# A two-layer streaming encoder step on one core: the first 24 projection units and their adaLN blocks rebuilt, and the dt unit in two passes

## The chip, the cores and the metric

The kernel runs on one core of a Trainium2 chip. The metric is the device time of one launch in microseconds (us). TensorE (PE) multiplies; VectorE (DVE), ScalarE (ACT) and GpSimd (POOL) do elementwise work; SyncE (SP) and POOL issue the DMAs.

## What is computed

A prompt of 256 tokens and a sample of 64 run together as T = 320 columns through two layers of width 2048. Layer 0 is a Mamba-2 mixer beside sliding-window attention, layer 1 a gated short convolution. All tensors are float32. What matters here is the head of layer 0:

```python
mod = jax.nn.silu(c) @ w_ada + b_ada
shift, scale, gate = jnp.split(mod[:, None, :], 3, axis=-1)
h = rms_norm(x, g_pre) * (1 + scale) + shift
z, xbc, dt_raw, q, k, v, g_att = jnp.split(h @ w_in, cuts, axis=-1)
dt = jax.nn.softplus(dt_raw + dt_bias)
```

`c` has one row for the prompt and one for the sample, so `mod` is a product of two rows with a 2048 x 6144 matrix (50 MB) per layer. The outputs of `h @ w_in` are cut into units of 128 columns.

## The kernel before

Activations lie transposed: 16 K tiles of 128 features by 320 tokens. A float32 product is made of three matmuls in a shorter format: weights and activations are split into a high and a low part (`split`, line 148: ScalarE copies the high part, VectorE subtracts), and `block` (line 152) issues high x high (line 169), high x low (line 170) and low x high (line 171) into one PSUM tile. A block of weights is 16 tiles of 128 x 128, in two halves of 8. Two halves are kept in a list of jobs ahead of TensorE (`LOOK`), so that the split runs before the matmuls; after every fourth tile a tick lets the side work go on.

The adaLN product has two forms. On TensorE (`ada_pe`, line 208) a quarter is a tile of 128 x 4 x 512 weights, 16 matmuls whose two useful rows of `cs` are padded to 32, so that four of them stand side by side in four column groups; four quarters are a block and give shift and scale for two K tiles, and `ada_end` (line 259) copies, transposes and adds. A float32 matmul shows as two records. On VectorE (`ada_side`, line 225) a block is summed in 16 steps, each of two multiply-adds on a 128 x 512 tile; `RATE_0` says how many steps a tick makes.

The first 24 units (k, v, and q and gate of two head pairs) need `h`, and `h` needs `mod`, which comes from 25 MB of weights. So they are not computed unit by unit: K is cut into pieces of 1, 1, 2, 4, 4, 4 tiles (`PIECES`), and each piece runs over all 24 units while the adaLN quarters of the next piece stand between the units. After a piece a unit's PSUM tile is added to its sum in SBUF (`start_unit`, line 395): by ScalarE (a copy, line 405) in piece 0, by VectorE (line 416) afterwards. The PSUM tiles are three banks of the pool `psm`.

K tiles 0 and 1 have adaLN weights of their own (`w0`, eight tiles of 512 KB), which `ada_first` (line 357) sums in two column groups, one for the shift and one for the scale. Tokens' squares are summed in two sums by ScalarE (line 325) and VectorE, joined, reduced over features with three matmuls (`by_token`), turned into 1/sqrt with integer operations and three rounds on VectorE (`rstd`, line 292) and spread with three matmuls (`r0b`). `modulate` (line 333) makes for each K tile: x times scale times rstd on VectorE (`mt`), the high half on ScalarE (`hh`, adds the shift), the low half on VectorE (`hl`).

A scheduler sets the order of each engine's instructions from the program's order and its own model; an engine then runs its queue strictly in that order. SP issues the weights' DMAs in its own fixed order; an issue waits until its buffer is free. The rest of the kernel, from line 459 on, runs units whole: attention, the dt unit (line 663: one unit with 32 useful columns, padded to 128), the SSM groups, the output products, and layer 1.

## Time and profile before

| | us |
|---|---|
| median of three runs (2165.87 to 2166.52) | 2166.22 |
| profiled execution, whole | 2171.02 |
| its span, first to last instruction | 2169.3 |
| TensorE busy in the span | 2124.2 (98%) |
| VectorE busy | 1412.8 (65%) |
| ScalarE busy | 884.9 (41%) |
| mean DMA rate over the span | 188 GB/s |

The profile is one execution. A matmul's busy time overlaps that of the next one, so busy shares of TensorE are upper bounds; starts tell its pace. Idle time is put down to what ended it. In stretches, PEclk is the share of the full clock of 2.4 GHz that TensorE was granted.

### The profile page before, as it was taken

How to read it: one execution, taken by the hardware profiler on the slowest of the kernel's cores; microseconds unless marked ns; L12 is line 12 of the kernel's file. 1: busy time of each engine (PE TensorE's matmuls, PEld its weight loads, DVE VectorE, ACT ScalarE, POOL GpSimd, SP SyncE). 2: the span in 40 equal slices, each digit the busy share in tenths (PEclk: the TensorE clock that was granted, in tenths of full speed). 3: DMA queues.
4: the chain of work that ended last, by engine and by line, in shares of the span. 5: the costliest groups of instructions: out<-in, count | busy, mean ns of one | idle time of the engine just before them, and what ended most of it. 6: DMA issues, size and time to landing. Idle time of an engine off the chain costs nothing.

```text
span 2169.3 us, 38007 instructions
## 1 busy us (share of the span) xinstructions
PE 2124.2 (98%) x15582; PEld 2056.5 (95%) x15582; DVE 1412.8 (65%) x2295; ACT 884.9 (41%) x1442; POOL 154.2 (7%) x370
## 2 busy tenths in 40 slices
PE   7999999999999999999999999999999999999997
PEld 6889999999999999997999999999999999999996
DVE  5876788897577878996755555555345554444444
ACT  5233455543465555355433333333333333333343
POOL 1000000000132223102000000000000000000001
PEclk9999999999999999999999999999999999999998
DMA  8886455466455556775554454545444454444441
GB/s 314 325 313 212 167 179 181 168 230 231 164 192 176 178 183 210 251 285 217 175 172 166 173 176 161 178 166 190 154 172 159 175 175 143 154 155 140 153 156 68
DMA packets 85758, 408.81 MB, mean 188 GB/s; under 512 B 10544, under 2 KB 11472, under 8 KB 46416
## 3 DMA queue, kind: packets, MB, share of 16 engines
q1 hardware_dynamic: 80496, 392.22, 51.8%
q0 software_dynamic: 5088, 14.16, 2.0%
q8 instruction: 122, 2.00, 0.4%
q14 instruction: 52, 0.43, 0.1%
HBM read 400.35 MB, written 5.99 MB: 187 GB/s over the span
## 4 chain that ended last, share of the span: by engine, by line
PE 90%; DVE 4%; DMA 2%; issue 1%; ACT 1%; POOL 1%; POOLq 0%; SPq 0%; DVEq 0%; ACTq 0%
PE pc L169 13%; PE pc L170 13%; PE pc L171 13%; PE px L169 3%; PE px L171 3%; PE px L170 3%; PE s L169 2%; PE s L171 2%; PE s L170 2%; PE pz L169 2%; PE pz L170 2%; PE poe L169 2%; PE pod L169 2%; PE pod L171 2%; PE poe L170 2%; PE pz L171 2%
## 5 line engine op out<-in xcount | busy, mean ns | idle before, releaser
L250 DVE SCALAR_TENSOR_TENSOR adac<-adas,cs,adac 128x512 f32<-128x512 f32 x420 | 300.2, 745 | 53.2 <-DMA adas<-in_wada 53.0
L956 POOL COPY ncc<-cp 128x2 f32<-128x2 f32 x32 | 6.0, 186 | 933.8 <-DVE cp L954 933.8
L219 PE MATMUL adap<-adaw,cs 128*32 128x128 f32 x1152 | 43.2, 284 | 3.5 <-DMA adaw<-in_wada 3.5
L219 PEld LDWEIGHTS adap<-adaw,cs 128*32 128x32 f32 x1152 | 31.6, 113 | 12.1 <-issue 6.3
L676 POOL COPY nca<-xp 128x3 f32<-128x3 f32 x24 | 22.3, 929 | 196.8 <-ACT xp L674 196.8
L961 DVE SCALAR_TENSOR_TENSOR cc<-cp,ccw,cc 128x322 f32<-128x322 f32 x64 | 35.3, 551 | 1.1
L512 ACT ACTIVATE pr<-s,mx 128x192 f32<-128x192 f32 (+2 forms) x80 | 29.8, 406 | 13.0 <-DVE mx L507 13.0
L710 ACT ACTIVATE sg<-sg,acum 128x128 f32<-128x128 f32 (+1 forms) x96 | 29.3, 376 | 12.9 <-POOL sg L702 12.9
L954 DVE TENSOR_TENSOR cp<-pc,u 128x256 f32<-128x256 f32 x31 | 13.2, 425 | 31.0 <-PE pc L171 30.8
L342 ACT ACTIVATE hh<-mt,mod 128x256 fp32r<-128x256 f32 x64 | 23.7, 419 | 20.9 <-DVE mt L341 20.7
L416 DVE TENSOR_TENSOR g<-s,g 128x320 f32<-128x320 f32 x40 | 19.0, 485 | 12.5 <-PE s L171 12.5
L681 DVE SCALAR_TENSOR_TENSOR cv<-xp,cw,cv 128x323 f32<-128x323 f32 x48 | 26.5, 552 | 0.6
L969 DVE TENSOR_TENSOR sgg<-pc,sgg 128x320 f32<-128x320 f32 x31 | 15.1, 488 | 17.4 <-PE pc L171 17.3
L879 DVE TENSOR_TENSOR oo<-poe,oo 128x320 f32<-128x320 f32 x16 | 7.9, 492 | 25.6 <-PE poe L171 25.6
L416 DVE TENSOR_TENSOR q<-s,q 128x320 f32<-128x320 f32 x40 | 18.9, 486 | 7.8 <-PE s L171 7.4
L702 POOL TENSOR_SCALAR_AFFINE_SELECT sg<-sg 128x512 f32<-128x512 f32 (+1 forms) x24 | 21.6, 911 | 30.0 <-DMA sg<-acs_b 29.9
L416 DVE TENSOR_TENSOR acc<-s,acc 128x320 f32<-128x320 f32 x32 | 15.3, 487 | 12.3 <-PE s L171 12.0
L363 PE MATMUL adaf<-w,cs 128*32 128x128 f32 x128 | 10.4, 311 | 12.8 <-ACT ss L325 12.6
L343 DVE SCALAR_TENSOR_TENSOR hl<-mt,mod,hh 128x256 fp32r<-128x256 f32 x64 | 21.5, 379 | 1.3 <-ACT hh L342 1.1
L363 PEld LDWEIGHTS adaf<-w,cs 128*32 128x32 f32 x128 | 8.1, 125 | 13.8 <-ACT ss L325 12.6
L263 ACT ACTIVATE adar_None<-adap 128x128 f32<-128x128 f32 x23 | 6.3, 273 | 34.8 <-PE adap L219 29.3
L512 ACT ACTIVATION_READ_ACCUMULATOR pr<-s,mx 128x1 f32 x80 | 17.9, 224 | 0.0
(2529 smaller groups left out, 8742.0 us busy)
## 6 DMA issues: line engine op xcount, KB each, us to landing
wc<-in_wio SPq DMA_DIRECT2D x124, 1024.0 KB, 4.9
adas<-in_wada SPq DMA_DIRECT2D x224, 256.0 KB, 5.9
adaw<-in_wada SPq DMA_DIRECT2D x36, 1024.0 KB, 7.0
wx<-in_wie SPq DMA_DIRECT2D x24, 1024.0 KB, 5.0
...
```

Source lines behind the costliest of these rows:

```text
L169: PE.matmul(ps, lhsT=wh[:, n, :], rhs=xh, start=st, stop=False)
L170: PE.matmul(ps, lhsT=wh[:, n, :], rhs=xl, start=False, stop=False)
L171: PE.matmul(ps, lhsT=wl[:, n, :], rhs=xh, start=False, stop=en)
L219: PE.matmul(ps[32 * q : 32 * q + 32, :], lhsT=cs[:, kt, :], rhs=(w[k] if raw else w[:, k, :])[:, 128 * q : 128 * q + 128], start=kt == 0, ...
L250: V.scalar_tensor_tensor(acc[s], w, c, acc[s], op0=ALU.mult, op1=ALU.add)
L342: S.activation(hi, t[:, a:b], AF.Identity, bias=sh)
L416: V.tensor_tensor(dst, ps, a, op=ALU.add)
L512: S.activation(pr[m][u // 2][:, u % 2, a : a + CH[c][2]], ss[m][u // 2][:, u % 2, a : a + CH[c][2]], AF.Exp, bias=mx[:, j, u : u + 1], sca ...
L676: G.tensor_copy(nca[:, ci, 0, :], xp[:, 256:259])
L681: V.scalar_tensor_tensor(cv, xp[:, n : n + 323], cw[:, ci, n : n + 1], cv, op0=ALU.mult, op1=ALU.add)
L710: S.activation(sgs[b][n][:, h, :], sgs[b][n][:, h, :], AF.Exp, bias=acum[0:nt, b, hd : hd + 1])
L961: V.scalar_tensor_tensor(cv, xp[:, m : m + 322], ccw[:, c, m : m + 1], cv, op0=ALU.mult, op1=ALU.add)
```

## The change

- **The first 24 units.** x is multiplied by rstd in place (`normal`); high half, and the low half's subtrahend, are then made from x with scale and shift on ScalarE (`shifted`; for K tiles 0 and 1 the subtrahend on VectorE). The adaLN quarters are fetched in halves of 512 KB into the buffers of the activations' pool and stand on TensorE in pairs, at places that `PAIRS` lists. Inside a half block the matmuls go K tile by K tile. PSUM tiles alternate over five banks of two pools. Units 20 to 23 stay in PSUM from piece 0 to piece 1, which begins with them.
- **TensorE's order** is that of the program from the first adaLN matmul to the end of the 24 units.
- **Tiles 0 and 1.** `ada_first` uses four column groups (even and odd K tiles apart), folded by a matmul with a doubled identity. The token sums are not joined but reduced in two steps; 1/sqrt uses ScalarE's square root.
- **Small loads** (key and value cache, sinks, convolution weights and others) are issued when the first unit of the last piece is done, and not at the start.
- **The dt unit.** The 32 useful columns' low parts are put beside their high parts (columns 32 to 63), so two passes, with the high and the low activations, give both sums; they are added where dt is transposed.
- The work pool has 19 buffers instead of 20; the side block begins in piece 2 at 0.36 steps per tick.

```diff
-SPE = 20
+SPE = 19
...
-RATE_0, RATE_A, RATE_B, RATE_C, RATE_D = 0.24, 0.55, 0.2, 0.6, 0.14
+RATE_0, RATE_A, RATE_B, RATE_C, RATE_D = 0.36, 0.55, 0.2, 0.6, 0.14
...
+    class PE:
+
+
+        @staticmethod
+        def matmul(*a, **k):
+            ins = nc.tensor.matmul(*a, **k)
+            return tc.keep_in_program_order(ins) if pin[0] else ins
...
+    def block(src, name, entries, h, pool=wp, order=None, parts=1):
...
-                for n, (get, kt, st, en, then) in enumerate(part):
+                for m, n in enumerate(order or range(8)):
+                    get, kt, st, en, then = part[n]
...
-    acc0 = sums[0]
-    V.tensor_tensor(acc0, acc0, sums[1], op=ALU.add)
...
+    def ada_first(t, ks, ps):
+
+        for kt in ks:
+            for q in range(2):
+                c = 64 * (kt % 2) + 32 * q
+                PE.matmul(ps[c : c + 32, :], lhsT=cs[:, kt, :],
+                          rhs=w0[4 * t + kt // 4][:, kt % 4, 128 * q : 128 * q + 128], start=kt < 2, stop=kt > 13)
+
+    pin[0] = True
+    ps0 = psa.tile([128, 128], F32, tag="ada", name="adaf0")
+    ada_first(0, range(4), ps0)
+    base = mean(by_token(sums[0], "ss0a", ones[:, 0:1]), D, "r0m")
+    ss = by_token(sums[1], "ss0t", ones[:, 0:1])
+    ada_first(0, range(4, 16), ps0)
+    rsp = rstd(ss, D, "r0", True, base)
+    ada_end(0, 0, ps0, 0)
...
+    def normal(kt, rs):
+        x = xin[kt // 4][:, kt % 4, :]
+        V.tensor_tensor(x, x, rs, op=ALU.mult)
+
+    def shifted(kt, h, late=True):
+
+        g, k = kt // 4, kt % 4
+        if k == 0:
+            h[0].append(gtile(f"hh0_{g}", F32R))
+            h[1].append(gtile(f"hl0_{g}", F32R))
+        t = stile([128, T], f"mt0_{kt}")
+        last = []
+        for s, a, b in SEGS:
+            sc, sh = mod[0][:, 1, kt, s : s + 1], mod[0][:, 0, kt, s : s + 1]
+            x, hi, lo = xin[g][:, k, a:b], h[0][g][:, k, a:b], h[1][g][:, k, a:b]
+            last.append((x, hi, lo, sc, sh, t[:, a:b]))
+            ih = S.activation(hi, x, AF.Identity, scale=sc, bias=sh)
+        for x, hi, lo, sc, sh, ts in last:
+            if late:
+                S.activation(ts, hi.bitcast(F32), AF.Identity, scale=-1.0, bias=sh)
+                il = V.scalar_tensor_tensor(lo, x, sc, ts, op0=ALU.mult, op1=ALU.add)
+            else:
+                V.tensor_scalar(ts, x, sc, sh, op0=ALU.mult, op1=ALU.add)
+                il = V.tensor_tensor(lo, ts, hi.bitcast(F32), op=ALU.subtract)
+        return ih, il
...
+    PAIRS = ((), (3, 10), (1, 6, 11, 16), (1, 6, 11, 16), (2, 9), ())
+    DEPTH = (2, 4, 4, 3, 3, 0)
+    first = [(0, b, sub) for b in range(1, 7) for sub in range(4)]
+    fetched, begun, carried = [], set(), {}
+
+    def ada_fetch(depth):
+
+        while first and len(fetched) < depth:
+            q = first.pop(0)
+            t = [act.tile([128, 2, 512], F32, tag="G", name=f"adaw{q[1]}_{q[2]}{m}") for m in range(2)]
+            for m in range(2):
+                nc.sync.dma_start(t[m], i["wada"][q[0], q[1], q[2]][:, 2 * m : 2 * m + 2, :])
+            fetched.append((q, [t[k // 2][:, k % 2, :] for k in range(4)]))
+
+    def ada_pair(depth):
+        for _ in range(2):
+            q, raw = fetched.pop(0)
+            ada_pe(*q, raw=raw)
+        ada_fetch(depth)
+        if q[2] == 3:
+            for kt in (2 * q[1], 2 * q[1] + 1):
+                shifted(kt, h0)
...
+            gate = G.dma_start(o["nk"][:, u, 0, :], kT[u][:, 128:256])
+            if u == 0:
+                with tc.issue_after(gate.ins):
+                    load_later()
...
+    normal(0, rsp)
+    behind = shifted(0, h0, False)
+    normal(1, rsp)
+    S.activation(rsb, rsp, AF.Copy)
+    banks = [0]
+
+    def bank(name):
+        banks[0] += 1
+        return mmps(name) if banks[0] % 5 < 3 else sps([128, T], name)
...
+        def then(n, ps, j=j, nxt=nxt, pairs=pairs, seen=seen):
+            c = seen[0]
+            seen[0] += 1
+            if not (j == 0 and n >= 20):
+                start_unit(n, ps, j == len(PIECES) - 1)
+            if j == 0 and c == 10:
+                ps1 = psa.tile([128, 128], F32, tag="ada", name="adaf1")
+                ada_first(1, range(16), ps1)
+                ada_end(0, 0, ps1, 1)
+                shifted(1, h0, False)
+                ada_fetch(DEPTH[1])
+            if c == 2 and nxt and j > 1:
+                for kt in range(nxt[0], nxt[0] + nxt[1]):
+                    normal(kt, rsb)
+            if c == 13 and j == 0:
+                for kt in (2, 3):
+                    normal(kt, rsb)
+            if pairs and c >= pairs[0]:
+                pairs.pop(0)
+                ada_pair(DEPTH[j])
+            if j == 2 and c == 8:
+                side["gen"], side["rate"] = ada_side([(0, 7)]), RATE_0
+            if j == 4 and c == 16:
                 finish_side()
-                modulate(xin, rsb, 0, *nxt, h0)
+                for kt in (14, 15):
+                    shifted(kt, h0)
...
+                keep = n >= 20 and j < 2
+                if keep and j:
+                    get = carried[n]
+                else:
+                    get = once(f"s{j}_{n}", bank)
+                    carried[n] = get
...
+            V.tensor_tensor(wh[:, :, 32:64], part[:, :, 0:32], wh[:, :, 0:32].bitcast(F32), op=ALU.subtract)
+
+            def mm(hf=hf, wh=wh):
+                ps = get()
+                for n in range(8):
+                    kt = 8 * hf + n
+                    for m in range(2):
+                        PE.matmul(ps[0:96], lhsT=wh[:, n, 0:96], rhs=h[m][kt // 4][:, kt % 4, :],
+                                  start=kt == 0 and m == 0, stop=kt == 15 and m == 1)
+                    if n % 4 == 3:
```

**TensorE at the start.** In the kernel before: `adaf` is tile 0's (218) or tile 1's (370) adaLN sum, `ss0t` the token sums, `r0b` the broadcast of rstd, `s_n` the PSUM tile of unit n, `hh` and `hl` the halves of the activations.

```order
L363 MATMUL adaf_218<-w_1_92,cs 32x128 x7
L313 MATMUL r0b<-r0d,ones 128x128 x2
L313 MATMUL r0b<-r0d,ones 128x64
L363 MATMUL adaf_218<-w_1_92,cs 32x128
L363 MATMUL adaf_218<-w_2_93,cs 32x128 x8
L363 MATMUL adaf_218<-w_3_94,cs 32x128 x8
L265 MATMUL adat_0_0_253<-ident,adar_0_0_251 128x64
L363 MATMUL adaf_370<-w_4_95,cs 32x128 x8
L363 MATMUL adaf_370<-w_5_96,cs 32x128 x5
L169 MATMUL s_0_319<-hh_0_296,ws00h_305 128x320
L169 MATMUL s_1_324<-hh_0_296,ws00h_305 128x320
L169 MATMUL s_2_329<-hh_0_296,ws00h_305 128x320
```

And after the change:

```order
L43 MATMUL adaf_193<-w_1_92,cs 32x128 x8
L43 MATMUL adaf_193<-w_2_93,cs 32x128 x8
L43 MATMUL adaf_193<-w_3_94,cs 32x128 x8
L43 MATMUL r0b<-r0d,ones 128x128 x2
L43 MATMUL r0b<-r0d,ones 128x64
L43 MATMUL adat_0_0_257<-fold,adar_0_0_255 128x64
L43 MATMUL s_0_320<-hh_0_286,ws00h_297 128x320
L43 MATMUL s_0_320<-hl_0_287,ws00h_297 128x320
L43 MATMUL s_0_320<-hh_0_286,ws00l_298 128x320
```

All of tile 0's adaLN stands ahead of the broadcast now, nothing of tile 1's stands ahead of the units, and the second matmul on unit 0 is the one with the low half.

**VectorE at the same place.** Before: `mt` is the scaled activation, `ws00l` and `ws01l` the low parts of the first weights, `hl` the low half of K tile 0.

```order
L341 SCALAR_TENSOR_TENSOR mt_0_298<-x_83,mod_134,rsb 128x256
L341 SCALAR_TENSOR_TENSOR mt_0_298<-x_83,mod_134,rsb 128x64
L150 TENSOR_TENSOR ws00l_306<-early_103,ws00h_305 128x1024
L150 TENSOR_TENSOR ws01l_310<-early_104,ws01h_309 128x1024
L343 SCALAR_TENSOR_TENSOR hl_0_297<-mt_0_298,mod_134,hh_0_296 128x256
L343 SCALAR_TENSOR_TENSOR hl_0_297<-mt_0_298,mod_134,hh_0_296 128x64
```

After: lines 404 are products of x with rstd, each of one K tile (`x_83` holds K tiles 0 to 3, `x_84` 4 to 7, `x_85` 8 to 11).

```order
L404 TENSOR_TENSOR x_83<-x_83,r0b 128x320
L424 TENSOR_SCALAR mt_0_288<-x_83,mod_139 128x256
L424 TENSOR_SCALAR mt_0_288<-x_83,mod_139 128x64
L169 TENSOR_TENSOR ws00l_298<-early_103,ws00h_297 128x512 x2
L404 TENSOR_TENSOR x_83<-x_83,rsb 128x320 x2
L404 TENSOR_TENSOR x_84<-x_84,rsb 128x320 x4
L404 TENSOR_TENSOR x_85<-x_85,rsb 128x320
L425 TENSOR_TENSOR hl_0_287<-mt_0_288,hh_0_286 128x256
L425 TENSOR_TENSOR hl_0_287<-mt_0_288,hh_0_286 128x64
L404 TENSOR_TENSOR x_85<-x_85,rsb 128x320 x2
L169 TENSOR_TENSOR ws01l_311<-early_104,ws01h_310 128x1024
```

Between the first low weights and the low half, seven products now stand; the second weights' low part has moved behind the low half.

**TensorE between units of piece 1.** Before, the third and the fourth quarter of block 1:

```order
L170 MATMUL s_15_683<-hl_0_297,ws11h_453 128x320
L219 MATMUL adap_1_508<-adaw_1_2_602,cs 32x128 x16
L171 MATMUL s_15_683<-hh_0_296,ws11l_454 128x320
L169 MATMUL s_16_692<-hh_0_296,ws12h_499 128x320
L170 MATMUL s_16_692<-hl_0_297,ws12h_499 128x320
L171 MATMUL s_16_692<-hh_0_296,ws12l_500 128x320
L169 MATMUL s_17_697<-hh_0_296,ws12h_499 128x320
```

After, the first two quarters, each from two half tiles:

```order
L43 MATMUL s_23_500<-hl_0_287,ws12h_370 128x320
L43 MATMUL s_23_500<-hh_0_286,ws12l_371 128x320
L43 MATMUL adap_1_526<-adaw_00_302,cs 32x128 x8
L43 MATMUL adap_1_526<-adaw_01_303,cs 32x128 x8
L43 MATMUL adap_1_526<-adaw_10_306,cs 32x128 x8
L43 MATMUL adap_1_526<-adaw_11_307,cs 32x128 x8
L43 MATMUL s_16_567<-hh_0_286,ws12h_370 128x320
L43 MATMUL s_16_567<-hl_0_287,ws12h_370 128x320
```

Where a quarter of 16 matmuls stood in the middle of a unit, two quarters now stand together between two units.

## Rows read from the trace of the kernel before

**Rows 1.** Section 1 and section 2 of the page of the whole execution: busy time of TensorE (PE) with its share of the span and its instructions, and its busy share in 40 equal slices of 54 us, in tenths.

```profile
PE 2124.2 (98%) x15582; PEld 2056.5 (95%) x15582; DVE 1412.8 (65%) x2295; ACT 884.9 (41%) x1442; POOL 154.2 (7%) x370
...
PE   7999999999999999999999999999999999999997
```

**Rows 2.** Busy time by stretch (us from the span's start; per engine busy us and instructions in brackets; then TensorE's granted clock, the share of the DMA engines, GB/s). The three stretches are the first two pieces of K, the other four pieces, and all that follows.

```profile
26.00:59.00 33.00, 30.34 (x309) 26.55 (x309) 20.45 (x44) 18.30 (x36) 0.00 (x0) 1.00 0.80 304
59.00:243.00 184.00, 178.73 (x1682) 167.18 (x1683) 135.38 (x247) 56.94 (x88) 5.42 (x10) 0.99 0.75 266
243.00:2169.00 1926.00, 1903.39 (x13487) 1853.51 (x13486) 1242.81 (x1960) 798.70 (x1295) 138.65 (x336) 0.99 0.51 177
```

**Rows 3.** The timeline of all engines from 11 to 27 us (start, length, engine, line, operation, names, count; in brackets the idle time before it and what ended it).

```profile
11.07 1.55 ACT L325 ACTIVATE ss<-x 128x320 f32<-128x320 f32 x4 [0.55 <-DMA x<-in_xT]
...
13.30 0.49 DVE L352 TENSOR_TENSOR ss<-ss,ss 128x320 f32<-128x320 f32 x1
...
13.85 1.44 PE L320 MATMUL ss0t<-ones,ss 128*128 128x1 f32 x6 [0.18 <-DVE ss L352]
...
15.33 0.16 DVE L297 TENSOR_SCALAR r0v<-ss0t 128x3 f32<-128x3 f32 x1 [1.53 <-PE ss0t L320]
...
18.10 1.54 PE L313 MATMUL r0b<-r0d,ones 128*128 128x128 f32 x6
...
19.58 2.28 PE L363 MATMUL adaf<-w,cs 128*32 128x128 f32 x34
...
21.89 0.27 ACT L263 ACTIVATE adar<-adaf 64x128 f32<-64x128 f32 x1 [1.77 <-PE adaf L363]
22.07 1.04 ACT L149 ACTIVATE ws00h<-early 128x1024 fp32r<-128x1024 f32 x1
...
22.59 0.22 DVE L269 TENSOR_SCALAR mod<-adat,bada 128x2 f32<-128x2 f32 x1 [4.15 <-PE adat L265]
...
23.70 1.22 DVE L150 TENSOR_TENSOR ws00l<-early,ws00h 128x1024 fp32r<-128x1024 f32 x1
...
23.96 0.73 ACT L342 ACTIVATE hh<-mt,mod 128x256 fp32r<-128x256 f32 x2
...
25.97 0.67 DVE L343 SCALAR_TENSOR_TENSOR hl<-mt,mod,hh 128x256 fp32r<-128x256 f32 x2
...
26.70 0.41 PE L170 MATMUL s<-hl,ws00h 128*128 128x320 f32 x1 [1.24 <-DVE hl L343]
```

**Rows 4.** The DMA view of the first 60 us: GB/s in 40 slices of 1.5 us, then issues by tile (issuing queue, count, KB of one, median us from issue to landing).

```profile
GB/s 0 96 301 414 414 401 356 385 167 279 418 418 426 412 421 412 415 407 412 426 421 426 396 399 408 455 352 55 71 246 382 202 431 66 0 55 295 415 366 321
...
w<-in_wada SPq DMA_DIRECT2D x8, 512.0 KB, 12.3
...
kT<-in_cachekT POOLq DMA_DIRECT2D x4, 64.0 KB, 6.3
```

**Rows 5.** The timeline again, three runs of equal instructions of VectorE (DVE) and ScalarE (ACT): squares added in SBUF, a unit's result copied out of PSUM, a unit's result added out of PSUM.

```profile
7.80 3.37 DVE L329 TENSOR_TENSOR ss<-ss,ss 128x320 f32<-128x320 f32 x8 [0.30 <-ACT ss L325]
...
27.30 3.43 ACT L405 ACTIVATE acc<-s 128x320 f32<-128x320 f32 x8 [2.60 <-PE s L171]
...
44.84 1.28 DVE L416 TENSOR_TENSOR acc<-s,acc 128x320 f32<-128x320 f32 x3
```

**Rows 6.** TensorE's instructions on the units' PSUM tiles (line, operation, count: min/median/max ns, first and last start).

```profile
L169 PE MATMUL s<-hh,ws20h x16: 304/309/415, 59.5 to 72.0; 128*128 128x320 f32 x16
...
L169 PE MATMUL s<-hh,ws54h x16: 309/309/309, 229.0 to 235.6; 128*128 128x320 f32 x16
...
L169 PE MATMUL s<-hh,ws55h x16: 309/309/309, 236.1 to 242.7; 128*128 128x320 f32 x16
```

**Rows 7.** TensorE's timeline around one adaLN quarter.

```profile
112.47 0.31 PE L169 MATMUL s<-hh,ws32h 128*128 128x320 f32 x1
112.71 1.08 PE L219 MATMUL adap<-adaw,cs 128*32 128x128 f32 x32
113.72 0.41 PE L170 MATMUL s<-hl,ws32h 128*128 128x320 f32 x1
113.97 0.31 PE L171 MATMUL s<-hh,ws32l 128*128 128x320 f32 x1
```

**Rows 8.** One group of TensorE's instructions from 59 to 243 us: the adaLN quarters (count, busy us, mean ns of one, idle before and its cause).

```profile
L219 PE MATMUL adap<-adaw,cs 128*32 128x128 f32 x640 | 23.1, 283 | 2.4 <-DMA adaw<-in_wada 2.4
```

**Rows 9.** Who TensorE waited for from 59 to 243 us, and then from 26 to 59 us (us in total, times, longest).

```profile
PE s L169 <- ACT hh L342: 3.1, 2, 1.6
PE adap L219 <- DMA adaw<-in_wada: 2.4, 3, 1.5
...
PE s L170 <- DVE hl L343: 1.2, 1, 1.2
```

**Rows 10.** Busy time by stretch, around the one fall of TensorE's clock in the first 250 us.

```profile
55.00:60.00 5.00, 3.37 (x31) 2.69 (x23) 4.73 (x16) 2.57 (x6) 0.00 (x0) 1.00 0.99 375
60.00:65.00 5.00, 5.00 (x45) 3.54 (x45) 3.27 (x8) 0.04 (x1) 0.00 (x0) 0.66 0.71 253
```

**Rows 11.** Who VectorE waited for from 59 to 243 us.

```profile
DVE adac L248 <- DMA adas<-in_wada: 2.0, 1, 2.0
DVE adac L250 <- DMA adas<-in_wada: 1.9, 2, 1.3
```

**Rows 12.** The instructions on the PSUM tile of the dt unit.

```profile
L169 PE MATMUL pdt<-hh,wdth x16: 308/309/412, 396.5 to 403.2; 128*128 128x320 f32 x16
```

More of the change, by code (lines that the diff above doesn't have):

```diff
@@ L261, in ada_end @@
         row = wk.tile([128, 128], F32, tag="arow", name=f"adar{l}_{b}_{one}")
[L262 to L263 removed]
+        S.activation(row, ps, AF.Copy)
         pt = sps([128, 128], f"adat{l}_{b}_{one}")
[L265 removed]
+        if one is None:
+            PE.transpose(pt, row, ident)
+        else:
+            PE.matmul(pt[:, 0:64], lhsT=row, rhs=fold, start=True, stop=True)
         got = pt.rearrange("p (q s) -> p q s", q=4)[:, :, 0:2]
@@ L321, in by_token, with mean @@
         return ps
+    def mean(ps, n, name):
+        b = wk.tile([128, 3], F32, tag="rb", name=name)
+        V.tensor_scalar(b, ps, 1.0 / n, EPS, op0=ALU.mult, op1=ALU.add)
+        return b
     def sumsq(acc, t, first, name):
@@ L344, in modulate @@
                                        op0=ALU.add, op1=ALU.subtract)
-    first = [(0, b, sub) for b in range(8) for sub in range(4)]
+    S.activation(wk.tile([128, 1], F32, tag="rt", name="table"), cs[:, 0, 0:1], AF.Sqrt, scale=0.0)
     sums = [stile([128, T], f"ss{n}") for n in range(2)]
@@ L618, in time_steps @@
         for b, (t0, nt) in enumerate(BL):
-            PE.transpose(pd[0:nt, b, :], dtr[:, t0 : t0 + nt], ident[0:32, 0:32])
+            PE.matmul(pd[0:nt, b, :], lhsT=dtr[:, t0 : t0 + nt], rhs=two, start=True, stop=True)
             V.tensor_copy(dt[0:nt, b, :], pd[0:nt, b, :])
@@ L661, in time_steps, with dt_unit @@
             G.dma_start(acs_b[b, :, 0:nt], at[:, t0 : t0 + nt])
-    unit(wie[16], "dt", h0, steps)
+    def dt_unit(src, h, then):
+        w = wp.tile([128, 16, 128], F32, tag="w", name="wdt")
+        nc.sync.dma_start(w, src)
+        get = once("pdt")
+        for hf in range(2):
+            wh = wp.tile([128, 8, 128], F32R, tag="wh", name=f"wdt{hf}")
+            part = w[:, 8 * hf : 8 * hf + 8, :]
+            S.activation(wh, part, AF.Copy)
+            V.tensor_tensor(wh[:, :, 32:64], part[:, :, 0:32], wh[:, :, 0:32].bitcast(F32), op=ALU.subtract)
[7 more added lines that the diff above has]
+                    if n % 4 == 3:
+                        yield
+                if hf:
+                    then(ps)
+            jobs.append(mm)
+            while len(jobs) > LOOK:
+                run()
+    dt_unit(wie[16], h0, steps)
     bTs, cTs, xss, zs = {}, {}, {}, {}
```

126 lines of the change are left out of this document (62 added, 64 removed).

## The prediction

> **What bounds the kernel now.** I read the page first, then busy time by stretch, then the waits and the timeline of the stage that is rebuilt. On the page TensorE is busy 98% of the span, and of the 40 slices only the first and the last fall below 9 tenths [rows 1]. By stretch it is idle 22.6 us in the 1926 us after the first 24 units (1.2%), 5.3 us in the 184 us of pieces 2 to 5, and 2.7 us in the 33 us of pieces 0 and 1 [rows 2]; before that it does nothing until token sums and adaLN weights are there [rows 3]. So a microsecond saved in the first 243 us reaches the end, as TensorE's queue is full behind it. The other engines count only where TensorE stands still for them: in piece 0 for the first low half of the activations (1.2 us), in pieces 2 to 5 for high halves (3.1 us) and for adaLN weights (2.4 us) [rows 9].
>
> "Busy" hides part of the loss. A 320-column matmul starts every 0.147 us (45 of them between the first and the last start of a half block: 6.6 us) [rows 6], so one unit times one K tile is 0.44 us. Pieces 2 to 5 hold 14 x 24 x 3 = 1008 of them, 148.2 us; they took 184 us. Twenty quarters (640 records, 32 each) stand in that stretch [rows 8]. One that stands whole costs 113.97 - 112.47 - 2 x 0.147 = 1.21 us; inside it a record follows another after (1.08 - 0.28)/31 = 0.026 us, so 32 records are 0.83 us and the two changes of operand about 0.38 us [rows 7, 8]. Twenty are 24.2 us. About 2 us I put down to the value transposes and the side block's few matmuls (an estimate from their number at a record's length). What is left, 184 - 148.2 - 24.2 - 2 = 9.6 us, is waits, quarters broken up between units, and one stretch at half clock: TensorE was busy 3.37 of 5 us, and in the next 5 us it was granted 0.66 on the mean, 1.2 GHz for two thirds of them: 5 x 0.34 = 1.7 us [rows 10].
>
> **The change, step by step.** The sum is made in the profiled execution: span 2169.3 us, 1.7 us around it, 2171.0 in all. The median of the plain runs is 2166.2; I take the differences over to it unchanged.
>
> *Start, -1.8 us.* The small loads on POOL's queue go. While they ran, two slices fell to 167 and 279 GB/s where the queue otherwise moves 412 to 426 [rows 4]. The last x tile landed at 11.05; I take 10.6, and four 0.52 MB weight tiles at 414 GB/s, 5.1 us, land by 15.7. Token sums ran from 13.85 to 15.3 and the arithmetic to the broadcast at 18.10, 2.8 us [rows 3]. Now the 0.49 us joining of the two sums goes, but a second set of three token matmuls stands ahead on TensorE; about 15.0. The square root from the table replaces two integer and two rounds of three small operations, 0.2 us apart each, by one of ScalarE and a reciprocal: about 1.9 us, so the broadcast is at 16.9 to 18.3. TensorE has finished tile 0's adaLN by then, where before 34 of its records stood behind the broadcast. x times rstd 0.5, mod 0.5, high half 0.73 [rows 3]: the first matmul can go at about 20, not 24.7. The second cannot: it needs the low half, and in VectorE's new order seven products stand ahead of it, whatever ScalarE has done. From 19.2: second product 0.42, shift 0.3, low weights 1.22, seven products at 3.37/8 = 0.42 [rows 5] 2.95, low half 0.67 [rows 3] gives 24.8. Before it was 26.70. So of nearly 5 us only 1.9 is kept.
>
> *Pieces 0 and 1, -1.6 us more.* 11 units x 0.44 bring TensorE to 29.7; tile 1's adaLN, now in four column groups, is 64 x 0.026 + 0.38 = 2.0 us: 31.8 (at two groups 34 records took 2.28 us [rows 3]). ScalarE has the row copy and a high half queued ahead of the copies of units 8 to 10, which hold three of the five banks. In the old start row copy to mod took 1.1 us [rows 3]; with 0.45 for the high half the copies begin at 33.4. Twelve at 3.43/8 = 0.43 [rows 5] and a short high half end at 38.9; the high part of the next weights, 1.04, and the low one, 1.22 [rows 3], at 41.1. TensorE is out of work by 39, so it waits some 2 us. Then VectorE bounds piece 1: five low parts at about 1.15, twenty additions at 1.28/3 = 0.43 [rows 5], two low halves 1.3 and mod: 16 us from 39.9, 55.9; TensorE's own 24 x 0.44 and two pairs would end at 55. I take 56 for the first matmul of piece 2; before it stood at 59.5 [rows 6]. Start and pieces together -3.5.
>
> *Pieces 2 to 5, -10.9 us.* Ten pairs replace twenty quarters: 1.21 + 0.83 = 2.04 each, 20.4 us against 24.2: -3.8. Of the 9.6 us of waits I keep 2.5. What hides the chain row copy, transpose, mod, high half, low half is now the last third of a piece, at least 6 units of 0.88 us, where before the first matmul of the next piece met it; and five banks cover four units of VectorE's lateness. The low half no longer needs a scale on VectorE (0.62 us per tile moves to ScalarE, which is busy 57 of 184 us [rows 2]). Bounds: all 9.6 stay (-3.8), or none (-13.4). 2.5 lies nearer to none, since the two named causes, the late high halves (3.1 us) and the late weights (2.4 us) [rows 9], are the ones that go: the chain starts earlier, and each pair's weights are fetched a pair ahead.
>
> The clock fell once after TensorE had stood still for a third of 5 us, and that cost 1.7 us [rows 10]. The new stop from 20 to 24.8 is longer than any stop behind the first matmul so far; I count no fall in the sum and one in the range. The Trainium skill (TensorE: Matmul & The Clock Gate, HAM oscillation — how this bites in real kernels) holds that a stop is paid twice in this manner; by that rule this forecast would be 1.7 us later.
>
> *dt unit, -2.4 us.* 16 matmuls per pass [rows 12]; two passes instead of three are 16 fewer at 0.147. Output rows do not change the pace of a 320-column stream in any row shown, so the bounds are 0 and -2.4. TensorE is full there, nothing hides it.
>
> *At nothing:* two more table loads of ScalarE (it is busy 41% [rows 1]); one buffer fewer in the work pool (bounds 0 and +2); the late small loads (they fall in piece 5, where DMA has room).
>
> Sum: -3.5 - 10.9 - 2.4 = -16.8; against the coarse steps of VectorE's order in pieces 0 and 1 I give back 1.8. Forecast 2166.2 - 15.0 = 2151.2 us, its own range 2146 to 2157.
>
> **Rivals.** *The early stops do not happen* (14%). If VectorE's seven products fit while the high half is made, and banks do not hold ScalarE, TensorE runs from 20.5: two tiles of 10.6, tile 1's 2.0, two pairs 4.1, 1.5 of changes: piece 2 at 49, 7 us earlier: 2144. For it: VectorE is idle then; against: in-order queues.
>
> *Weights come too late* (16%). Pieces 1 and 2 take 12 quarters and 4.7 MB of unit weights, 17.3 MB, in the 46 us from 39 to 85: 376 GB/s. From 26 to 59 us the queue gave 304 [rows 2], which needs 57 us; some 3 us of it are prefetched: +8, 2159. Against: slices at 412 to 426 with tiles of this size [rows 4]. The Trainium skill (DMA: Bandwidth & Descriptors, Bandwidth) wants 1 MiB per transfer and gives 341 GB/s for one; the halves are 0.5 MB. By that figure 17.3 MB are 51 us, and the time would be about 2155.
>
> *Given back later* (8%). If the next 900 us are idle like pieces 2 to 5 (5.3 of 184 us, 2.9%) and not like now (1.2%) [rows 2], since pools, banks and side block stand otherwise, 15 us return: 2166. Against: TensorE's order behind the stage is nearly unchanged.
>
> *Fixed order makes it slower* (7%). TensorE can no longer take another unit while one waits. In piece 3 VectorE has side-block operations ahead of the unit additions, and the fourth side tile is issued on SP behind four half quarters that wait for a pair's buffers. VectorE waited up to 2.0 us for such tiles [rows 11]. If each of the last 13 waits 2.0 us beyond the five banks' cover, 26 us come back: 2177. It decides from 1.2 us each.
>
> **Chances.** Forecast 55%. Faster by over 0.2% (4.3 us, about what measurement can tell from no change): the forecast, the first rival and most of the second, 84%. Within: a rest of the second and the third, 9%. Slower: the fourth, 7%. Range 2144 to 2162: it leaves out half of the first rival, the fourth and most of the third.
>
> **What would show it.** A first low matmul at 24 to 25.5 after one lone high one at 20; ScalarE-bound copies until 39 and a 2 us stop before the next tile's third matmul; piece 2 at 54 to 58; pairs of 2.0 us; the stage's end at 229 to 233 instead of 243; 32 dt matmuls. It is wrong if TensorE waits for adaLN weights more than 5 us in all, or if the stage's gain is not seen at the end.

## The result and the profile after

| us | before | after |
|---|---|---|
| median (runs) | 2166.72 (6) | 2175.2 (6) |
| lowest and highest | 2165.87, 2172.33 | 2172.17, 2177.01 |
| profiled execution, whole | 2171.02 | 2174.95 |
| its span | 2169.3 | 2173.3 |

The ratio is 1.0035, 95% interval 1.0022 to 1.0048: the change makes the kernel 0.35% slower. Forecast were 2151.2 us, range 2144 to 2162, and 7% for slower.

The page of the kernel after, busy time and TensorE's share in slices (before: [rows 1]):

```profile
PE 2116.0 (97%) x15577; PEld 2054.3 (95%) x15577; DVE 1409.4 (65%) x2275; ACT 899.1 (41%) x1474; POOL 157.5 (7%) x371
...
PE   6999999999999999999999999999999999999997
```

Busy time of the kernel after by stretch (before: [rows 2]), then around its two stops:

```profile
26.00:59.00 33.00, 30.16 (x339) 27.69 (x339) 21.26 (x43) 19.30 (x42) 0.00 (x0) 0.95 0.84 326
59.00:243.00 184.00, 174.66 (x1689) 167.68 (x1690) 124.80 (x214) 69.17 (x111) 12.92 (x25) 1.00 0.72 254
...
22.00:29.00 7.00, 3.75 (x13) 3.40 (x14) 7.00 (x17) 2.41 (x5) 0.00 (x0) 0.52 1.03 408
...
843.00:880.00 37.00, 31.88 (x216) 29.42 (x215) 25.36 (x42) 18.43 (x40) 11.16 (x21) 0.91 0.64 207
```

TensorE is *less* busy in pieces 2 to 5 than before (174.7 against 178.7 us), though the same work is done in the same time: it stands still longer. And there are two places at a lower clock, in the start and behind 865 us.

First and last starts of four units' matmuls in the kernel after: the first of piece 2, the first behind the 24 units, the first of the output product with the side block beside it (pos), the first of the convolution layer's products (pc):

```profile
L43 PE MATMUL s<-hh,ws20h x16: 305/309/412, 59.0 to 70.2; 128*128 128x320 f32 x16
...
L43 PE MATMUL pq<-hh,wq20h x16: 309/309/414, 242.0 to 250.5; 128*128 128x320 f32 x16
...
L43 PE MATMUL pos<-ysh,wos0h x16: 308/309/392, 847.9 to 855.4; 128*128 128x320 f32 x16
...
L43 PE MATMUL pc<-hh,wc10h x16: 309/309/309, 1048.7 to 1055.3; 128*128 128x320 f32 x16
```

and two of them before:

```profile
L169 PE MATMUL pos<-ysh,wos0h x16: 309/309/392, 849.9 to 857.5; 128*128 128x320 f32 x16
...
L169 PE MATMUL pc<-hh,wc10h x16: 309/309/309, 1044.7 to 1051.3; 128*128 128x320 f32 x16
```

Against before ([rows 6] for 59.5 and, from the last start there, 243) the lead is 0.5 us at piece 2, 1.1 at the end of the 24 units, 2.1 at pos, and at pc it is a lag of 3.9, which stays to the end. So nearly all of the stage's gain is missing, and 6.0 us are lost between 848 and 1049.

**The 24 units.** I sorted pieces 2 to 5 by the time from each TensorE record's start to the next one's. Quarters with their changes of operand and waits fell from 30.3 to 20.8 us (20.4 were forecast). But the steps into and out of the row transposes (adat) rose from 1.1 to 5.9, those of the value transposes (vp) from 2.0 to 4.9, and unit matmuls from 150.1 to 151.2. Sum: -0.65. The five longest waits of TensorE after, 59 to 242 us, and the group of the adaLN quarters from 59 to 243 us (its last number is the idle time ahead of it; before: [rows 8]):

```profile
PE adat_None L48 <- ACT adar_None L282: 3.8, 6, 1.8
PE vp L48 <- DVE vT L504: 2.5, 4, 0.7
PE s L43 <- DVE ws30l L169: 1.4, 1, 1.4
PE s L43 <- DVE ws31l L169: 1.0, 1, 1.0
PE s L43 <- DVE q L504: 0.8, 1, 0.8
...
L43 PE MATMUL adap<-adaw,cs 128*32 128x128 f32 x640 | 19.5, 274 | 0.0
```

Waits for high halves and adaLN weights [rows 9] are gone; their place is taken by transposes. TensorE's timeline after, a pair with its transpose, and a group of value transposes:

```profile
109.28 1.95 PE L43 MATMUL adap<-adaw,cs 128*32 128x128 f32 x64
111.63 0.33 PE L48 MATMUL adat_None<-ident,adar_None 128*128 128x128 f32 x1 [0.40 <-ACT adar_None L282]
...
205.07 0.31 PE L43 MATMUL s<-hh,ws51l 128*128 128x320 f32 x1
205.97 0.55 PE L48 MATMUL vp<-ident,vT 128*128 128x128 f32 x3 [0.58 <-DVE vT L504]
```

Before, the scheduler had put other matmuls between an adaLN block's last quarter and its transpose, and nothing stood still:

```profile
96.17 0.31 PE L169 MATMUL s<-hh,ws30h 128*128 128x320 f32 x1
96.32 0.28 PE L265 MATMUL adat_None<-ident,adar_None 128*128 128x128 f32 x1
96.35 0.39 PE L170 MATMUL s<-hl,ws30h 128*128 128x320 f32 x1
```

**Behind 848 us.** TensorE's and ScalarE's timeline after:

```profile
864.24 0.42 PE L43 MATMUL adap<-adac,es 128*32 128x128 f32 x8 [0.94 <-DVE adac L270]
...
869.49 0.48 PE L48 MATMUL adat_None<-ident,adar_None 128*128 128x128 f32 x1 [4.18 <-ACT adar_None L282]
...
864.92 0.53 ACT L947 ACTIVATE ea<-ea 128x384 f32<-128x384 f32 x1 [4.65 <-issue]
...
867.71 1.56 ACT L865 ACTIVATE sg<-sg,acum 128x128 f32<-128x128 f32 x5
869.18 0.26 ACT L282 ACTIVATE adar_None<-adap 128x128 f32<-128x128 f32 x1
```

The side block's sum is ready at 864.7. Its row copy on ScalarE, 0.26 us long, runs at 869.18: ahead of it in ScalarE's queue stand `ea`, which started at 864.92, and ten more operations behind that. The view names nothing that `ea` waited for, but its broadcast, issued at 857.22 while side tiles and a weight tile were loading, landed at 864.85. The Trainium skill (PSUM — Partial Sum Buffer, Engine vs sequencer instructions) calls ScalarE's queue a strict FIFO; the row agrees. Before, this block ended 34 matmuls earlier in the order, and its row copy stood ahead of `ea`:

```profile
860.29 0.27 ACT L263 ACTIVATE adar_None<-adap 128x128 f32<-128x128 f32 x1
860.45 1.86 ACT L710 ACTIVATE sg<-sg,acum 128x128 f32<-128x128 f32 x6
862.21 0.52 ACT L792 ACTIVATE ea<-ea 128x384 f32<-128x384 f32 x1
```

The granted clock was 1.2 GHz from 868.76 for 6.83 us (0.91 on the mean over the 37 us from 843). The first 0.7 us of that lie in the stop of 4.18 us; the 6.1 us that TensorE then ran at half clock cost it 3.0 us. The Trainium skill (TensorE: Matmul & The Clock Gate, HAM oscillation — how this bites in real kernels) holds that a stop is paid again in the clock; here 4.2 and 3.0.

### The profile page after: what moved, and what is told of

Same layout as the page of the kernel before. It is cut to its first block, busy times and chain, and to the rows that moved or that the text cites. A ratio compares the mean times of both kernels' runs of the same rounds, so it can differ in the third digit from the quotient of the medians.

```text
span 2173.3 us, 38039 instructions
## 1 busy us (share of the span) xinstructions
PE 2116.0 (97%) x15577; PEld 2054.3 (95%) x15577; DVE 1409.4 (65%) x2275; ACT 899.1 (41%) x1474; POOL 157.5 (7%) x371
## 4 chain that ended last, share of the span: by engine, by line
PE 93%; DVE 2%; DMA 1%; ACT 1%; issue 1%; POOL 0%; SPq 0%; POOLq 0%; ACTq 0%; DVEq 0%
PE pc L43 40%; PE px L43 8%; PE s L43 7%; PE pq L43 5%; PE pod L43 5%; PE poe L43 5%; PE pz L43 5%; PE poa L43 5%; PE pot L43 2%; PE pos L43 2%; PE adap L43 2%; PE c L43 1%; PE o L43 1%; PE pt L48 1%; PE st L43 1%
## 5 line engine op out<-in xcount | busy, mean ns | idle before, releaser
L43 PE MATMUL adap<-adaw,cs 128*32 128x128 f32 x1152 | 37.6, 275 | 1.9 <-DMA adaw<-in_wada 1.9
L1124 DVE TENSOR_TENSOR sgg<-pc,sgg 128x320 f32<-128x320 f32 x31 | 15.2, 490 | 19.7 <-PE pc L43 19.5
L836 DVE SCALAR_TENSOR_TENSOR cv<-xp,convaw,cv 128x323 f32<-128x323 f32 x48 | 26.6, 553 | 0.5
L504 DVE TENSOR_TENSOR q<-s,q 128x320 f32<-128x320 f32 x40 | 18.5, 489 | 12.8 <-PE s L43 12.7
L637 ACT ACTIVATION_READ_ACCUMULATOR pr<-s,mx 128x1 f32 x80 | 17.8, 222 | 0.0
L418 ACT ACTIVATE hh<-x,mod 128x256 fp32r<-128x256 f32 (+1 forms) x32 | 15.0, 513 | 6.6 <-DVE mod L298 4.8
L43 PE MATMUL adaf<-w,cs 128*32 128x128 f32 x128 | 5.8, 347 | 12.1 <-DMA w<-in_wada 12.1
L1092 POOL TENSOR_TENSOR x<-x,oo 128x320 f32<-128x320 f32 x8 | 7.7, 985 | 131.7 <-DVE oo L1087 131.7
L628 DVE TENSOR_REDUCE mx<-s 128x2 f32<-128x384 f32 (+2 forms) x40 | 16.3, 468 | 1.1 <-PE s L43 1.0
L834 ACT ACTIVATE cv<-xp,convab,convaw 128x323 f32<-128x323 f32 x24 | 15.9, 664 | 2.0
```

Of the source, the lines that this page charges most:

```text
L43: ins = nc.tensor.matmul(*a, **k)
L504: V.tensor_tensor(dst, ps, a, op=ALU.add)
L628: V.tensor_reduce(mx[:, j, 2 * h : 2 * h + 2], ss[m][h][:, :, a : a + CH[c][2]], axis=AX.X, op=ALU.max)
L637: S.activation(pr[m][u // 2][:, u % 2, a : a + CH[c][2]], ss[m][u // 2][:, u % 2, a : a + CH[c][2]], AF.Exp, bias=mx[:, j, u : u + 1], sca ...
L834: S.activation(cv, xp[:, 0:323], AF.Identity, scale=cw[:, ci, 0:1], bias=cb[:, ci : ci + 1])
L836: V.scalar_tensor_tensor(cv, xp[:, n : n + 323], cw[:, ci, n : n + 1], cv, op0=ALU.mult, op1=ALU.add)
```

## Experiments

Medians are of 5 to 12 executions; "before again" is a single one. All times in the table are us of TensorE's first start in the profiled execution; "pos to pc" is the stretch with the side blocks of the next layer.

| kernel | first low matmul | piece 2 | end of 24 units | pieces 2-5 | pos to pc | median | ratio |
|---|---|---|---|---|---|---|---|
| before | 26.70 | 59.46 | 243.12 | 183.7 | 194.8 | 2166.72 | 1 |
| before again | 27.08 | 61.16 | 240.91 | 179.8 | 196.1 | (2170.26) | |
| after | 25.87 | 58.97 | 241.98 | 183.0 | 200.8 | 2175.2 | 1.0035 |
| ends later (e6) | 25.99 | 57.38 | 238.15 | 180.8 | 201.8 | 2172.09 | 1.0023 |
| no fixed order (e5) | 28.88 | 62.66 | 239.23 | 176.6 | 200.8 | 2172.84 | 1.0025 |
| side before flush (e2) | 25.92 | 59.05 | 242.39 | 183.3 | 194.4 | 2171.61 | 1.0021 |
| dt alone (e3) | 26.49 | 59.34 | 241.01 | 181.7 | 194.2 | 2168.60 | 1.0006 |
| 19 buffers alone (e7) | 26.68 | 60.08 | 241.33 | 181.3 | 193.5 | 2167.49 | 1.0000 |
| side as before (e8) | 26.84 | 60.89 | 245.27 | 184.4 | 195.0 | 2169.53 | 1.0009 |
| + products (e10) | 23.39 | 57.10 | 238.73 | 181.6 | 192.9 | 2168.03 | 1.0001 |
| + ends later (e9) | 23.20 | 55.76 | 237.89 | 182.1 | 193.4 | 2166.15 | 0.9992 |
| fixed in two pieces (e12) | 23.63 | 55.77 | 233.94 | 178.2 | 193.3 | 2159.12 | 0.9959 |
| + softmax one tick (e13) | 23.45 | 55.55 | 234.66 | 179.1 | 193.5 | 2158.35 | 0.9952 |
| e13, side as changed (e14) | 23.56 | 55.87 | 233.75 | 177.9 | 202.4 | 2165.27 | 0.9991 |

The ratios are to runs of before made beside each kernel (medians 2166.72 to 2167.45); their intervals reach about 0.0009 to each side (up to 0.0014 for after, e12 and e13). One profile is not read finer than 3 us: the kernel after and e8 have the same instructions up to 243 us and end the stage 3.3 us apart. About 1 us of that is the clock in the start. In e8 the matmuls of the first units start 0.267 us apart until 32.2 us, the pace of the half clock (its profile has no clock record ahead of 32.16); in the kernel after they do so from 25.9 to 29.1.

```profile
31.54 0.47 PE L43 MATMUL s<-hh,ws00h 128*128 128x320 f32 x1
31.80 0.47 PE L43 MATMUL s<-hl,ws00h 128*128 128x320 f32 x1
...
32.41 0.30 PE L43 MATMUL s<-hl,ws00h 128*128 128x320 f32 x1
32.55 0.31 PE L43 MATMUL s<-hh,ws00l 128*128 128x320 f32 x1
```

Read over several profiles, the rebuilt stage is not shown to gain anything: with the old one (before, before again, e3, e7) the 24 units end at 240.9 to 243.1 us, with the changed one (after, e2, e8) at 242.0 to 245.3.

**Before again.** 

> The kernel before, profiled once more. Its first profile lies 4.3 us above its median and holds three short stretches at half clock (at 60.8, 893.7 and 1013.1 us, 3.41 us long, about 1.7 us lost in each). Theory: the last two come in some executions only, so this profile has one or none of them, ends 2 to 4 us earlier, and the milestones up to 840 us agree with the first within 0.5 us. Rival: they belong to the kernel, and the span is 2169 again.

By its numbers the rival: span 2168.6, and the falls of the clock came again (at 890.9 and, 6.83 us long, at 1010.4); the milestones up to 840 us differ by up to 2.2 us. But this execution took 2170.26, where the plain ones beside it have a median of 2167.14, so both profiles of before lie 3 to 4 us above the median. Of those 29 plain executions, the ones with a mean granted clock of 0.996 took 2165.3 to 2167.3 us, the ones with 0.993 2169.4 to 2172.1; the two profiles had 0.994 and 0.993. In e3 and e7, whose profiled executions took 2167.74 and 2166.95, no fall came at these places. So the profile that the forecast rests on held two falls, 3.4 us, that executions near the median need not have.

**Row and value transposes later (e6).**

```diff
-            ada_pe(*q, raw=raw)
+            row = ada_pe(*q, raw=raw)
...
+            due.append([2, end_block])
...
+            due.append([3, turn_values])
```

> The changed kernel with the row transposes (adat) of pieces 1 to 4 written two unit ends, and the value transposes (vp) three unit ends, behind the place where they stand now; everything else as changed. Theory A (TensorE in fixed order stands still at each transpose, because its input is still being copied by ScalarE or added by VectorE): in the changed kernel the ten steps into adat and vp took 5.39 + 3.75 us, and a step is about 0.15; so about 7.6 us go, pieces 2 to 5 take 175 to 177 us instead of 183.0, the stage ends at 234 to 236 instead of 242.0, and if nothing changes behind it the time is about 2168 (ratio 1.000 to 1.001 instead of 1.0035). Rival B (the waits only move: the matmuls that run meanwhile use up the banks, or the late modulation meets the next piece): the stage still ends at 240 or later and the ratio stays at 1.0025 to 1.005.

Between the two. Steps at adat fell from 5.9 to 1.6, at vp from 4.9 to 2.0: 7.1 us went, as theory A has it. But unit matmuls rose from 151.2 to 155.1 and quarters from 20.8 to 21.8; TensorE now waits in fixed order for the next late thing (the four longest waits):

```profile
PE s L43 <- DVE ws40l L169: 1.3, 1, 1.3
PE s L43 <- DVE ws22l L169: 1.2, 1, 1.2
PE s L43 <- ACT ws30h L166: 1.1, 1, 1.1
PE s L43 <- DVE ws31l L169: 1.0, 1, 1.0
```

Of the 7.1 us, 2.2 remain in pieces 2 to 5. With a start of piece 2 that is 1.6 us earlier the stage ends 3.8 us earlier; the median is 3.1 less, with overlapping intervals of the ratios.

**No fixed order (e5).** `pin[0] = True` is left out.

> The changed kernel without its fixed order on TensorE: the scheduler may move the matmuls of the stage; nothing else is changed. The scheduler moves the value transposes behind each other, but leaves the row transposes close to their pairs. Theory A (waits at the transposes are what eats the gain): only the vp waits go, about 3 of the 3.75 us, the row transposes keep most of 5.39: stage end 238 to 240.5, ratio 1.0015 to 1.003. Rival C (the fixed order as a whole costs, since TensorE can't take another unit while one waits): the stage ends at 235 or earlier, ratio below 1.001. Rival D (the fixed order gains, and without it switches between quarters and units come back): stage end at 243 or later.

The stage end of theory A, but not for its reason: the start was 3.7 us later than in the kernel after, and the stage itself took 176.6 us, the shortest of all, with unit matmuls at 148.3, which is their bare pace (1008 times 0.147 is 148.2). That is rival C's mechanism, hidden by a bad start: the first low matmul came only at 28.88, and the matmuls behind it started 0.267 us apart until 33.3. It led to e12.

**The side blocks' places.** Two runs. First only the order of two lines:

```diff
-    flush()
-    pin[0] = False
     side["gen"] = ada_side(...)
     side["rate"] = RATE_A
+    flush()
+    pin[0] = False
```

> The changed kernel with the next side block's generator set ahead of the flush, as in the kernel before, so that its blocks end about 30 matmuls earlier in the order; everything else as changed. Theory A2 (the loss between 848 and 1045 us comes from where the side blocks end: at 865 us the row copy stands on ScalarE behind operations that wait for a broadcast by DMA, TensorE waits 4.2 us and then runs at half clock for 6.8 us): the wait and the half clock at 865 to 876 go, from there on the differences to the kernel before fall from +3.9 to -1 to -3, and the ratio is 0.9995 to 1.0005. Rival B2 (the loss there is not due to the side blocks' places but to something else that the change moved): TensorE loses 4 us or more between 848 and 1045 again, and the ratio stays above 1.0025.

Then with `side["due"] -= 0.15` behind the rate, which puts each later block's end at the matmul where it was before:

> The changed kernel, but the next side block's generator is set ahead of the flush, as before, and its count lowered by 0.15 so that every later side block ends at the same matmul as in the kernel before; behind the dt unit the order of TensorE's work is then that of the kernel before. Theory A2 (what is lost between 848 and 1045 us comes from the order there): stage end 242 as in the changed kernel, 3 to 4 us ahead of the kernel before at 848, no wait above 2 us between 848 and 1045 and the lead kept to the end; ratio 0.9975 to 0.9995. Rival B2 (it comes from the shift in time itself or from the buffers): 3 us or more are lost again between 848 and 1045, ratio 1.001 or more.

From pos to pc they take 194.4 and 195.0 us, like before, where every kernel with the changed places takes 200.8 to 202.4. The wait in e8, 843 to 1045 us:

```profile
PE c L43 <- ACT hh L374: 1.2, 1, 1.2
PE adat_None L48 <- ACT adar_None L282: 1.0, 1, 1.0
```

The stretch is as A2 said; the totals are not (1.0021 and 1.0009 instead of 1.0005 and less), since the stage ahead had given no lead to keep. e8 is 5.7 us faster than the kernel after by medians. In the profile of before the same stretch held the two falls of the clock; in e3, e7, e9, e10, e12 and e13, with the old places and no fall there, it takes 192.9 to 194.2 us. Against that the changed places cost the kernel after 6.6 to 7.9 us, and its stop and its half clock behind 865 us, 4.2 + 3.0, are that much. The edits move all side blocks at once; in e5 and e6 the stop at that transpose is only 2.9 and 1.9 us, and more of the loss is time at half clock (in e5 two stretches of 3.41 us, in e6 one of 6.83 and one of 3.41).

**The dt unit alone (e3), and 19 buffers alone (e7).**

> The kernel before with the dt unit in two passes and one buffer fewer in the work pool (19, for the room that the two new tiles need); nothing else changed. The prediction's term: 16 matmuls at 0.147 fewer, 2.4 us, and the buffer 0 to 2: ratio 0.9989 to 0.9998. Rival (what a shift of 2.4 us changes at the side blocks outweighs it, as in the changed kernel): ratio 1.0005 to 1.003, with a new wait of over 2 us behind 840 us.

> The kernel before with one buffer fewer in the work pool (19), nothing else. The prediction's bounds: 0 to +2 us. Theory E (the buffer costs nothing): ratio 0.9995 to 1.0005. Rival (it is what the run with the dt unit alone paid): ratio 1.0005 to 1.001 with a wait for a side tile or an operation that held the buffer.

The buffer costs nothing that can be measured. The dt unit gains nothing (the ratio is in the rival's range, but between 848 and 1041 us no wait is above 1.3 us): its records take 4.6 us instead of 7.0, but from wq37's first matmul to woa0's TensorE takes 55.4 us instead of 54.8. TensorE's wait there, and ScalarE's timeline, of e3:

```profile
PE pz L169 <- ACT wz00h L149: 1.6, 1, 1.6
```

```profile
396.57 1.28 ACT L514 ACT_TABLE_LOAD   x1 [1.19 <-DVE es L510]
...
401.99 0.28 ACT L519 ACTIVATE es<-es 128x12 f32<-128x12 f32 x1
402.09 1.12 ACT L149 ACTIVATE wz00h<-wz 128x1024 fp32r<-128x1024 f32 x1
```

ScalarE makes the second high half of the next unit only behind a block of exponentials. Before, with the third pass of dt, TensorE waited for nothing there; without it TensorE arrives first and waits 1.6 us. What else is lost of the 2.4 us was not traced.

**The products of x (e10).** On top of e8:

```diff
+            if kt > 1:
+                st_.enter_context(tc.issue_after(behind[1].ins))
             V.tensor_tensor(x, x, rs, op=ALU.mult)
```

> As the run with the side blocks' places of before, and the fourteen products of x (from tile 2 on) may only be issued behind the first tile's low half. Theory S (VectorE's order sets the first low matmul, and what is won there reaches piece 2): first low matmul at 23 to 23.5 us instead of 25.87, piece 2 starts at 56 to 57 instead of 58.97, stage end and time 2 to 3 us earlier than in that run. Rival R (ScalarE's copies and VectorE's work in pieces 0 and 1 set piece 2 whatever TensorE's start): piece 2 starts at 58.3 or later and the time changes by under 0.7 us.

Theory S for the start: the first low matmul and piece 2 (57.10) come out as it says. TensorE's start in e10, and VectorE's seven products with the low half behind them in the kernel after:

```profile
22.53 0.42 PE L43 MATMUL s<-hh,ws00h 128*128 128x320 f32 x1 [2.44 <-ACT hh L421]
23.39 0.63 PE L43 MATMUL s<-hl,ws00h 128*128 128x320 f32 x1 [0.44 <-DVE hl L428]
```

```profile
22.44 2.91 DVE L404 TENSOR_TENSOR x<-x,rsb 128x320 f32<-128x320 f32 x7
25.25 0.56 DVE L425 TENSOR_TENSOR hl<-mt,hh 128x256 fp32r<-128x256 f32 x2
```

The clock is at half for 3.41 us instead of 6.83, but the half clock is hardly cheaper: TensorE works through 3.0 us of it here and 3.2 in the kernel after, where the rest fell into the stop. Piece 2 starts 1.9 us earlier than in the kernel after; by medians e10 is 1.5 less than e8, where 2 to 3 were expected, and with intervals that overlap, so the gain in time is not shown.

**All three (e9).**

> The changed kernel with all three edits: side blocks where they ended before, products behind the first low half, row transposes two and value transposes three unit ends later. If theories A, A2 and S hold and add up: piece 2 at 55 to 57, stage end at 233 to 236, dt unit another 2.4, no loss between 848 and 1045 us; 9 to 12 us ahead of the kernel before, ratio 0.9945 to 0.996. If the stage's gain is always given back behind it (rival): ratio 0.999 or more.

Piece 2 and the stretch behind 848 are as expected, the end of the 24 units is not (237.9): with transposes out of the way unit matmuls again take 156.5 us, 1.7 of it one fall of the clock at 90.8. The ratio of 0.9992 is the rival's, its reason is not: in the profile the lead over before is 6.1 us at pos and 7.5 at pc, so nothing is given back behind the stage. Later transposes only hand the wait on.

**Fixed order in two pieces only (e12).** On top of e10: `pin[0] = j < 2` at the head of each piece.

> The changed kernel with the side blocks where they ended before and the products of x behind the first low half, and with the fixed order of TensorE kept for pieces 0 and 1 only; in pieces 2 to 5 the scheduler may move matmuls. Theory C (in a fixed order TensorE pays each lateness of ScalarE and VectorE at the place where it arises; in the run with no fixed order at all the stage itself took 176.6 us, and only its start was late): piece 2 starts at 56 to 58, pieces 2 to 5 take 175 to 178 us instead of 181 to 184, stage end at 232 to 235, ratio 0.996 to 0.9985. Rival (the stage was quicker there only because it began later and the weights were waiting): pieces 2 to 5 take 180 us or more and the ratio is that of the run with all three edits, 0.999.

Theory C. Unit matmuls take 147.7 us, their bare pace (151.2 in e10), adat and vp 1.8 and 2.0 (4.5 and 4.9). But quarters rise from 20.8 to 26.5: the scheduler breaks the pairs up again, and of 9.1 us that the waits give back 5.7 are paid there. The fixed order had kept the pairs whole; what it cost was more. All of TensorE's waits from 55 to 234 us that the view lists:

```profile
PE s L43 <- DVE ws31l L169: 1.0, 1, 1.0
PE adat_None L48 <- ACT adar_None L282: 0.4, 1, 0.4
PE s L43 <- ACT ws34h L166: 0.3, 1, 0.3
```

The median is 8.9 below e10's and 8.3 below that of before beside it (ratio 0.9959, 0.9946 to 0.9971). The profiles of e10 and e12 are only 5.0 apart; e10's was the fastest of its 11 runs, and what the others lose more was not seen, so a little under half of the 8.9 us is not accounted for by the traces.

**Softmax one tick later (e13).** `wait[0] += 1` ahead of the dt unit.

> As the run with the fixed order in two pieces, with the attention tasks one tick later from the dt unit on, so that ScalarE makes the second high half of the unit behind dt ahead of the 14 exponentials and not behind them. Theory D (the dt unit's 2.4 us are lost at once, because ScalarE's block of exponentials, which the third pass covered, now meets the next unit's weights): the wait of pz for wz00h (1.3 to 1.6 us) goes, and from the dt unit's first matmul to poa's first one TensorE takes 44 to 45.3 us instead of 46.5; 1.2 to 2.5 us earlier in all. Rival (the block meets another unit's weights): 46 us or more, no gain.

The wait for wz00h is gone. The expectation's stretch was badly chosen, for attention matmuls moved ahead of dt's first one; from wq37 to woa0 it is 53.45 us (53.15 in e14), 55.18 in e12 and 54.83 before. So the dt unit is worth 1.4 to 1.7 us against before once ScalarE's order lets it. By medians 0.8 less than e12, with overlapping intervals; it is the fastest kernel here (0.9952, 0.9938 to 0.9966).

**e13 with the changed places (e14).**

> As the run with the attention one tick later, but with the side block's generator set behind the flush, as in the changed kernel; its blocks then end where the changed kernel's do. Theory A2 (the places of the side blocks cost the changed kernel 5.5 to 7 us between pos's first and pc's first matmul, by themselves): that stretch takes 199 to 202 us instead of 193.5, and the time is 4.5 to 7 us longer, 2163 to 2165.5, ratio 0.9975 to 0.999. Rival (those places only cost where the stage ahead ends as it does in the changed kernel): the stretch takes under 196 us, ratio 0.9945 to 0.9965.

As A2 said: 202.4 us, 6.9 us longer by medians, with the same wait, here 5.5 us. The clock was at half for 6.83 us again, 4.0 of them inside the stop, and once more for 3.41 us from 1006.9.

```profile
PE adat_None L48 <- ACT adar_None L282: 5.5, 1, 5.5
```

## Why the prediction was wrong

By terms, in the two profiled executions (forecast, then found; the dt unit from wq37's first matmul to woa0's):

| | forecast | found |
|---|---|---|
| start | -1.8 | -0.8 |
| pieces 0 and 1 | -1.6 | +0.3 |
| pieces 2 to 5 | -10.9 | -0.65 |
| dt unit | -2.4 | +0.5 |
| given back | +1.8 | |
| the rest up to pos | 0 | -1.4 |
| pos to pc | 0 | +6.0 |
| sum | -15.0 | +4.0 |

- **The step that failed most is "Pieces 2 to 5, -10.9 us".** Its first half was right: pairs and earlier fetches brought quarters and their waits to 20.8 us, and the adaLN weights never came late. What failed is "Of the 9.6 us of waits I keep 2.5": I asked which old waits would go, and not which instruction in the new fixed order stands directly behind the one that feeds it. The transposes stood in the sum "at a record's length", about 2 us; they took 10.8 in all, and e6 shows that moving them only lets the next late operand be seen. e12 removes both, and pays part of it in quarters. No run came near the 10.9 us: e12's 178.2 us for pieces 2 to 5 are 5.5 below this profile of before and 1.6 to 3.5 below before again, e3 and e7.
- **The rival "Fixed order makes it slower"** had the sign and its reason, that TensorE can't take another unit, but the wrong place. VectorE's waits for side tiles did not fall on unit additions; row copies, vT additions and low weights were late. That its 2177 us lies near the measured 2175.2 is luck: most of the loss against the forecast came from other places than the 13 unit additions it counted.
- **"At nothing" missed the side blocks' places.** The diff moves the generator behind the flush, so most blocks end 30 to 122 matmuls later, the one at 865 us 34. I had it only in the rival "Given back later", by an average over 900 us. The places of the blocks are worth 6 to 7 us (e2, e8, e14); that it is mainly the queue order at this one block is read from the stop there.
- **The dt unit**: the 16 matmuls did go. The prediction asked for the cover of its other edits and here only wrote "nothing hides it"; it did not ask what the third pass covered. That 96 output rows keep the pace was right: 32 matmuls start within 4.6 us in e3.
- **Start**: the mechanism was right, seven products ahead of the low half, 2.91 us for 2.95 forecast (e10 takes them away). The token sums were there at 15.9 for 15.0 forecast, and the broadcast came at 18.5 to 19.5 and not 16.9 to 18.3. The operand of its matmuls was ready at 17.8, but tile 0's adaLN stands ahead of them on TensorE and ran until then:

```profile
15.80 2.79 PE L43 MATMUL adaf<-w,cs 128*32 128x128 f32 x48
18.52 1.02 PE L43 MATMUL r0b<-r0d,ones 128*128 128x128 f32 x6
...
17.14 0.68 DVE L339 TENSOR_SCALAR r0d<-ident,r0y 128x128 f32<-128x128 f32 x3
```

- **Pieces 0 and 1**: the clock was at half from 22.25, when the first high matmul began, to 29.08. TensorE ran 3.2 us of that behind the stop, which cost 1.6 us; the two rows of the table miss by 2.9 together, 1.0 in the start and 1.9 here. The fall stood in the range and not in the sum.
- **"I take the differences over to it unchanged"**: the profiled execution of before lay 4.3 us above the median. Between the two profiles the forecast missed by 19 us, between the forecast time and the median after by 24; the difference of 5 us is this step.
- **Weights late**, 16%, did not happen: with 512 KB halves the queue moved 408 GB/s in the start, and the quarters of pieces 2 to 4 had 0.0 us idle ahead of them. The Trainium skill (DMA: Bandwidth & Descriptors, Bandwidth) gives 341 GB/s for a transfer of 1 MB; with several in flight the trace does not bear that out. (In the rival itself, 51 us with the 3 us of prefetch that it counts would have been about 2153 and not 2155.)

Not varied alone, so without a price of their own, are the late small loads, the four column groups of tiles 0 and 1 and the side block's rate.
